# The context's up product in native fp32, and the S5 table sums moved from GpSimd to VectorE

## The chip, the core and the metric

The kernel runs on one core of one Trainium2 chip. The metric is the device time of one execution in microseconds (us), taken as the median of several runs. Engines are named as the profile names them: PE is the matrix engine (TensorE) and PEld its weight loads, DVE is VectorE, ACT is ScalarE, POOL is GpSimd, SP is SyncE, whose queue starts nearly all DMA transfers.

## What is computed

One layer over 1024 latent tokens and 256 context tokens, model width 1024, hidden width 2816. The part that matters is the first half-step SwiGLU on the context tokens, and the tables of the S5 scan that are built beside it:

```python
def half_step_ffn(x, mods, g_pre, g_post, w_gu, w_down):
    shift, scale, gate = mods
    h = modulate(rms_norm(x, g_pre), shift, scale)
    g, u = jnp.split(h @ w_gu, 2, axis=-1)
    y = (jax.nn.silu(g) * u) @ w_down
    return x + 0.5 * gate * rms_norm(y, g_post)
...
x = half_step_ffn(x, mods[0:3], ...)          # latent tokens
ctx = half_step_ffn(ctx, mods_c[0:3], ...)    # context tokens
```

The S5 tables are complex products of powers of `lam_bar` with the input matrix B and the output matrix C (`s5_discretise`, `s5_states` and `s5_readout` in the reference). They are needed later, by the scan over the latent tokens.

## The kernel before

The work runs in stages. First the latent up product (`g_lat`), then the context's up product (`g_ctx`, line 980), then the latent down product (`d_lat`, line 794), the context's down product, the mixer with the S5 pairs, and the second half-step. Side work is given out in small steps between the main steps: each main loop calls `step` (line 122), which advances a generator. During `g_ctx` that generator is `prep` (line 1760): 15 steps of `s5_prep` (line 1285), then loads of stored latent sums (`s_fetch`, seen as `z<-sd`), then the rest of `s5_prep`. The framework orders each engine's instructions by program order and by its own estimate of when they are ready; each engine, and SP's queue, then runs its list strictly in that order.

Matmuls mostly use a split scheme. `split` (line 157) turns an fp32 tensor into two tiles of type float32r: the high part is a rounded copy that ACT makes, the low part is the remainder, which DVE subtracts. `proj` (line 574) then makes each product of three matmuls: high by high, high by low, low by high.

`g_ctx` runs over 22 blocks of 128 hidden columns. For each block it needs two weight blocks of 1024 by 128 (512 KB each), one for the gate and one for the up half. `wcols` loads each into one of four buffers (`wrs`, tile `wr`), and splits it into two tiles of the pool `w` (six buffers, so three pairs). The raw buffer is free again once both halves of the split are made. With 8 blocks of the contraction, 22 blocks, two halves and three matmuls there are 1056 matmuls with 256 columns. The normalised context comes from `prenorm_g` (line 467), which splits it as well: `chi` and `clo`, four tiles of the pool `z`. Results leave through an ACT `Silu` and a DVE product, and are stored (`scd<-z`).

`s5_prep` makes four table blocks with `cmul` (line 1324: six DVE or POOL operations on 128x1024), and four with two groups of three (lines 1379 to 1386). Of each four, the odd ones run on POOL. After each `cmul` the matrix engine makes 16 small products with 32 columns, in native fp32, and 16 transposes. The tables go out as `pd<-z`, and the Toeplitz blocks through many small transfers, `gd<-z` and `td<-gd`. In the trace every recorded operation has line 51, which is a wrapper, so groups go by tile.

Of the kernel before, what the change touches and what calls it, by code (L numbers as in the profile page):

```python
# [10 lines left out]
F32R = mybir.dt.float32r  # L11
# [5 lines left out]
P = 128  # L17
D = 1024
KT = D // P
DFF = 2816  # L20
NF = DFF // P
NT = 1024
NC = 256
# [45 lines left out]
class Kernel:  # L69
# [397 lines left out]
    def prenorm_g(self, xs, a, b, hi, lo, wait=0):  # L467
        ss = self.t(self.sm, [P, 4], "ss")
        for k, x in enumerate(xs):
            self.square(ss, k, x)  # L470
            if k % SQ == SQ - 1:
                yield
        for _ in range(wait):
            yield
        r = self.rsq(ss[:, : len(xs)])
        yield
        for k, x in enumerate(xs):
            self.ts(x, x, r[:, k : k + 1])
            if k % SQ == SQ - 1:
                yield  # L480
        for _ in range(wait):
            yield
        _, one = self.blocks(xs, a, b)
        for kt in range(KT):
            h = self.t2()[:, : len(xs) * P]
            one(kt, h)
            self.split(hi(kt), lo(kt), h)
            yield

    def hop(self, x):  # L490
# [486 lines left out]
            t0 += n  # L977


    def g_ctx(self, wgu, hi, lo, fills):  # L980
        cols = lambda f: [self.wcols(wgu, f * P + q * DFF) for q in range(2)]
        nxt = cols(0)
        for f in range(NF):
            ws = nxt
            if f + 1 < NF:
                nxt = cols(f + 1)
            self.step(fills)
            if f % 4 == 0:
                s = self.z([P, 4, NC])
            pg, pu = self.ps(), self.ps()  # L990
            self.proj(pg[:, :NC], ws[0], hi, lo)
            self.proj(pu[:, :NC], ws[1], hi, lo)
            sg = self.t2()[:, :NC]
            self.nc.scalar.activation(sg, pg[:, :NC], AF.Silu)
            self.mul(s[:, f % 4, :], sg, pu[:, :NC])
            if f % 4 == 3 or f == NF - 1:
                n = (f % 4 + 1) * NC
                self.load(self.scd[f // 4][:, :n], s.rearrange("p k n -> p (k n)")[:, :n])
# [286 lines left out]
    def s5_prep(self):  # L1285
        nc, i = self.nc, self.i
        pl = nc.gpsimd
        slot = lambda shape: self.t(self.zp, shape, "z")
        crs = [slot([P, 4, 2, 64]) for _ in range(2)]
        for k, nme in enumerate(("ssm_c_re", "ssm_c_im")):  # L1290
            for d in range(2):
                self.load(crs[k][:, :, d, :], i[nme][0, d].rearrange("(b g) h p -> (g h) b p", b=4))
        pw, br_ = slot([P, 2, 2, T8, 32]), slot([P, 2, 32, H])
        self.load(pw.rearrange("p w r t a -> p (w r t a)"), self.pwd)
        self.load(br_.rearrange("p r a h -> p (r a h)"), self.brd)
        yield
        czp = [slot([P, 32, 2, H]) for _ in range(2)]
        ct = slot([P, 2, 32, H])
        for k in range(2):
            pl.memset(czp[k], 0.0)  # L1300
        for _ in range(4):
            yield
        for k in range(2):
            pt = self.ps()
            for b in range(4):
                self.tr(pt[:, b * P : (b + 1) * P], crs[k][:, b].rearrange("p d n -> p (d n)"), P)
            self.ts(ct[:, k].rearrange("p a h -> p (a h)"), pt, 1.0 - 2 * k)
            for d in range(2):
                r = slice(64 * d, 64 * d + 64)
                nc.scalar.activation(czp[k][r, :, d, :], ct[r, k], AF.Copy)  # L1310
            yield
        kt_ = slot([P, G, 32])
        pdv = self.pd.rearrange("a p w -> p a w")
        shp = [P, 8, T8, H]

        def power(w, r, gs):
            return pw[:, w, r, :, gs].rearrange("p t a -> p a t").unsqueeze(3).to_broadcast(shp)

        for o in range(4):
            gs = slice(8 * o, 8 * o + 8)  # L1320
            xr, xi, xt = slot(shp), slot(shp), slot(shp)
            b0 = br_[:, 0, gs, :].unsqueeze(2).to_broadcast(shp)
            b1 = br_[:, 1, gs, :].unsqueeze(2).to_broadcast(shp)
            self.cmul(xr, xi, power(0, 0, gs), power(0, 1, gs), b0, b1, xt, pl if o % 2 else None)
            yield
            pk = self.ps()
            for a in range(8):
                for r, xx in ((0, xr), (1, xi)):
                    nc.tensor.matmul(
                        pk[:, 32 * a : 32 * a + 32],  # L1330
                        xx[:, a].rearrange("p t h -> p (t h)"),
                        czp[r][:, 8 * o + a].rearrange("p q h -> p (q h)"),
                        start=r == 0,
                        stop=r == 1,
                    )
            nc.vector.tensor_copy(kt_[:, gs, :], pk[:, :256].rearrange("p (a n) -> p a n", n=32))
            yield
            for r, xx in ((0, xr), (1, xi)):
                ev = slot([P, 8, P])
                for b in range(2):  # L1340
                    pt = self.ps()
                    for a in range(4):
                        self.tr(
                            pt[:, a * P : (a + 1) * P],
                            xx[:, 4 * b + a].rearrange("p t h -> p (t h)"),
                            P,
                        )
                    nc.scalar.activation(
                        ev[:, 4 * b : 4 * b + 4, :], pt.rearrange("p (a n) -> p a n", n=P), AF.Copy
                    )  # L1350
                c0 = BO + 256 * r
                self.load(
                    pdv[:, 4 * o : 4 * o + 4, c0 : c0 + 256], ev.rearrange("p (a q) n -> p a (q n)", q=2)
                )
                yield

        lag0 = slot([H, G, H])
        self.load(lag0, kt_[112:128, :, 0:H])
        self.add(lag0, lag0, kt_[0:16, :, H:])
        for t in range(T8):  # L1360
            r = slice(t * H, t * H + H)
            if t < 7:
                self.load(self.gd[:, :, 14 - t], kt_[r, :, 0:H])
            if t > 0:
                self.load(self.gd[:, :, 7 - t], kt_[r, :, H:])
        self.load(self.gd[:, :, 7], lag0)
        yield
        for t in range(T8):
            r = slice(t * H, t * H + H)
            self.load(self.td[r], self.gd[:, :, 7 - t : 15 - t].rearrange("h g l k -> h g (l k)"))  # L1370
            if t % TY == TY - 1:
                yield
        for o in range(4):
            gs = slice(8 * o, 8 * o + 8)
            mr, mi, xt = slot(shp), slot(shp), slot(shp)
            prb, pib = power(1, 0, gs), power(1, 1, gs)
            cr_ = ct[:, 0, gs, :].unsqueeze(2).to_broadcast(shp)
            ci_ = ct[:, 1, gs, :].unsqueeze(2).to_broadcast(shp)
            e = pl if o % 2 else None
            self.mul(mr, cr_, prb, e)  # L1380
            self.mul(xt, ci_, pib, e)
            self.add(mr, mr, xt, e)
            yield
            self.mul(mi, ci_, prb, e)
            self.mul(xt, cr_, pib, e)
            self.sub(mi, mi, xt, e)
            for r, m in ((0, mr), (1, mi)):
                c0 = CO + 256 * r
                self.load(
                    pdv[:, 4 * o : 4 * o + 4, c0 : c0 + 256], m.rearrange("p (a q) t h -> p a (q t h)", q=2)  # L1390
                )
            yield
# [218 lines left out]
    def run(self):  # L1611
        nc, i = self.nc, self.i
# [3 lines left out]
        xs = i["x"][0].rearrange("(c t) d -> t c d", t=T8)  # L1616
# [7 lines left out]
        xt = [self.z() for _ in range(4)]  # L1624
# [32 lines left out]
        pt = self.ps()  # L1657
# [12 lines left out]
        h = self.hops(stages, bl, hb)  # L1670
# [35 lines left out]
        q, a = norm2(), accs2()  # L1706
# [30 lines left out]
            yield from self.s5_params()  # L1737

        hc = []
        chi = lambda k: hc[k // 4][:, k % 4, :]  # L1740
        clo = lambda k: hc[2 + k // 4][:, k % 4, :]

        def side():
            ct = [self.z() for _ in range(2)]
            for b in range(2):
                self.load_block(ct[b], cblk(b))
            hc.extend(self.z([P, 4, NC], dt=F32R) for _ in range(4))
            yield from self.prenorm_g(ct, self.modc[1, 1], self.modc[0, 1], chi, clo, 3)

        self.fill = fill()  # L1750
        self.lag = 0
# [19 lines left out]

        self.floor = ()
        self.fill = prep()
        self.g_ctx(i["ffn1_w_gu"][0], chi, clo, FC)
        self.drain()


# [184 lines left out]
        p = evac(2, acc)  # L1962
# [70 lines left out]
FC = 2  # L2033
# [53 lines left out]
```

## Time and profile before

| | |
|---|---|
| median of 3 runs | 2115.37 us (2113.56 to 2116.61) |
| profiled execution | 2112.9 us |
| span in its trace, first to last instruction | 2111.1 us |
| mean granted clock of TensorE | 0.964 of full speed |
| PE busy | 91% of the span |
| DVE, ACT, POOL busy | 77%, 39%, 11% of the span |
| `g_ctx`, first to last matmul | about 542.6 to 720.2 us from the start |

The profile comes from one execution. Its busy shares are means over stages, so a change in one stage has to be read from that stage's window. The time of a matmul in a group is longer than its share of the engine, since matmuls overlap; the spacing in a dense run tells its price.

### The profile page before, as it was taken

To read this page: it belongs to the slowest core of one execution; us is meant where nothing else is said; L and a number is where in the kernel's file an instruction comes from. 1 tells how busy PE (TensorE), PEld (TensorE's weight loads), DVE (VectorE), ACT (ScalarE), POOL (GpSimd) and SP (SyncE) were. 2 spreads that over 40 slices of the span, in tenths; PEclk is the share of its full clock that TensorE was granted. 3 is DMA by queue.
4 is the path that set the end of the run, shared out by engine and by line. 5 is a ranking of instruction groups with operands and counts; after the bars stand their busy time and mean duration, and the time that the engine had idled before them with its cause. 6 is when DMAs were issued, how large, how long until landed. Compare 5 with 4: busy or idle time off the path is not lost.

```text
span 2111.1 us, 25392 instructions
## 1 busy us (share of the span) xinstructions
PE 1913.8 (91%) x9018; PEld 1589.2 (75%) x9018; DVE 1631.6 (77%) x2791; ACT 816.2 (39%) x1416; POOL 228.8 (11%) x136
## 2 busy tenths in 40 slices
PE   5789898898899979999998789998799999999997
PEld 4568776686899857877887578886688888887775
DVE  6789998998866878798549998478875555577977
ACT  5433222333333334566531113337233333334443
POOL 0000000051336200000003552010000000000000
PEclk9989999999999999999999999999899999999999
DMA  8357552244579979276684443233552222167554
GB/s 301 99 161 238 161 181 78 86 154 150 170 216 271 348 285 309 88 267 250 184 241 169 146 141 114 69 104 116 167 185 88 90 90 82 64 254 273 206 184 160
DMA packets 338443, 366.20 MB, mean 173 GB/s; under 512 B 43216, under 2 KB 250764, under 8 KB 338316
## 3 DMA queue, kind: packets, MB, share of 16 engines
q1 hardware_dynamic: 336012, 356.19, 51.6%
q10 hardware_dynamic: 2304, 8.39, 1.0%
q8 instruction: 71, 1.16, 0.2%
q14 instruction: 56, 0.46, 0.1%
HBM read 293.45 MB, written 73.12 MB: 174 GB/s over the span
## 4 chain that ended last, share of the span: by engine, by line
PE 54%; DVE 30%; DMA 7%; issue 4%; ACT 3%; POOL 1%; SPq 1%; DVEq 0%; ACTq 0%; POOLq 0%
PE ps L51 54%; DVE t L51 11%; DVE z L51 7%; DVE w L51 6%; DVE tb L51 5%; DMA wr<-in_ffn_w_gu 2%; DMA wr<-in_ffn_w_down 1%; DMA tb<-in_w_ada 1%; ACT w L51 1%; ACT z L51 1%; ACT t L51 1%; DMA z<-sd 1%; SPq L51 1%; DVE sy L51 0%; DVE red L51 0%
## 5 line engine op out<-in xcount | busy, mean ns | idle before, releaser
L51 PE MATMUL ps<-z,w 128*128 128x512 f32 (+1 forms) x5712 | 1241.0, 378 | 94.4 <-ACT w L51 43.8
L51 PEld LDWEIGHTS ps<-z,w 128*128 128x128 f32 x5712 | 1016.7, 194 | 296.4 <-ACT w L51 50.1
L51 PE MATMUL ps<-w,w 128*128 128x512 f32 x1848 | 430.7, 393 | 18.8 <-DVE w L51 14.4
L51 PEld LDWEIGHTS ps<-w,w 128*128 128x128 f32 x1848 | 346.8, 189 | 99.9 <-DVE w L51 22.0
L51 ACT ACTIVATE w<-wr 128x512 fp32r<-128x512 f32 (+1 forms) x286 | 215.3, 758 | 375.4 <-PE ps L51 289.7
L51 DVE TENSOR_TENSOR w<-wr,w 128x512 fp32r<-128x512 f32 (+1 forms) x280 | 258.7, 929 | 86.1 <-ACT w L51 78.6
L51 ACT ACTIVATE w<-t 128x512 fp32r<-128x512 f32 x308 | 187.2, 627 | 289.2 <-DVE t L51 206.7
L51 DVE TENSOR_TENSOR w<-t,w 128x512 fp32r<-128x512 f32 x308 | 212.0, 698 | 60.0 <-ACT w L51 59.7
L51 DVE TENSOR_TENSOR t<-t,ps 128x512 f32<-128x512 f32 x150 | 102.2, 683 | 59.7 <-PE ps L51 59.2
L51 ACT ACTIVATE w<-z 128x512 fp32r<-128x512 f32 x110 | 69.3, 630 | 147.4 <-PE ps L51 143.8
L51 DVE TENSOR_TENSOR t<-wr 128x512 f32<-128x512 f32 x148 | 99.7, 686 | 29.0 <-DMA wr<-in_ffn_w_down 13.5
L51 ACT ACTIVATE t<-ps 128x512 f32<-128x512 f32 (+2 forms) x135 | 73.7, 548 | 108.4 <-PE ps L51 107.0
L51 DVE TENSOR_TENSOR z<-z,z 128x512 fp32r<-128x512 f32 (+3 forms) x127 | 104.9, 860 | 9.3 <-ACT z L51 5.0
L51 DVE SCALAR_TENSOR_TENSOR tb<-tb,scol 128x1024 f32<-128x1024 f32 x77 | 98.0, 1281 | 9.3 <-DMA tb<-in_w_ada 9.1
L51 DVE TENSOR_TENSOR w<-z,w 128x512 fp32r<-128x512 f32 x110 | 75.6, 688 | 27.4 <-ACT w L51 27.0
L51 POOL TENSOR_TENSOR z<-z,z 128x1024 f32<-128x1024 f32 x24 | 84.5, 3539 | 80.6 <-PE ps L51 44.9
L51 ACT ACTIVATE t<-z 128x1024 bf16<-128x1024 f32 (+3 forms) x132 | 75.2, 605 | 43.6 <-DVE z L51 30.3
L51 ACT ACTIVATE t<-t 128x512 f32<-128x512 f32 (+1 forms) x81 | 50.6, 625 | 104.6 <-DVE t L51 99.4
L51 PE MATMUL ps<-z,t 128*128 128x512 f32 x384 | 87.8, 389 | 1.1 <-ACT t L51 1.1
L51 PEld LDWEIGHTS ps<-z,t 128*128 128x128 f32 x384 | 72.0, 188 | 16.4 <-ACT t L51 1.5
L51 POOL TENSOR_TENSOR tb<-tb 128x512 f32<-128x512 f32 x24 | 34.9, 1465 | 447.9 <-DVE w L51 428.7
L51 ACT ACTIVATE z<-z 128x512 fp32r<-128x512 f32 (+2 forms) x76 | 47.9, 672 | 71.8 <-DVE z L51 66.1
(122 smaller groups left out, 1418.6 us busy)
## 6 DMA issues: line engine op xcount, KB each, us to landing
wr<-in_ffn_w_gu SPq DMA_DIRECT2D x156, 512.0 KB, 4.4
wr<-in_ffn_w_down SPq DMA_DIRECT2D x198, 256.0 KB, 4.1
tb<-in_w_ada SPq DMA_DIRECT2D x64, 512.0 KB, 4.7
sd<-z SPq DMA_DIRECT2D x44, 512.0 KB, 4.8
z<-sd SPq DMA_DIRECT2D x88, 256.0 KB, 5.2
z<-in_w_ada SPq DMA_DIRECT2D x24, 512.0 KB, 6.3
wr<-in_ffn_w_down SPq DMA_DIRECT2D x22, 512.0 KB, 4.9
wr<-in_w_in SPq DMA_DIRECT2D x20, 512.0 KB, 3.8
```

The source lines that it names most:

```text
L51: r = f(*a, **kw)
```

## The change

The context's up product takes the fp32 weights and the fp32 activations directly: one native fp32 matmul in place of three float32r ones, no split of the weights and none of the normalised context. The weights are read by the matmuls out of the four `wr` buffers. In `s5_prep` the odd table blocks now run on DVE like the even ones. (POOL keeps its blocks in `s5_params`, line 1248, and its work elsewhere.)

```diff
@@ prenorm_g
         for kt in range(KT):
-            h = self.t2()[:, : len(xs) * P]
+            h = hi(kt) if lo is None else self.t2()[:, : len(xs) * P]
             one(kt, h)
-            self.split(hi(kt), lo(kt), h)
+            if lo is not None:
+                self.split(hi(kt), lo(kt), h)
@@ g_ctx
-    def g_ctx(self, wgu, hi, lo, fills):
-        cols = lambda f: [self.wcols(wgu, f * P + q * DFF) for q in range(2)]
-        nxt = cols(0)
+    def g_ctx(self, wgu, h, fills):
+        def cols(f, q):
+            raw = self.wr().rearrange("p (k n) -> p k n", n=P)
+            c0 = f * P + q * DFF
+            self.load(raw, wgu[:, c0 : c0 + P].rearrange("(k p) n -> p k n", p=P))
+            return raw
+
+        nxt = [cols(0, q) for q in range(2)]
         for f in range(NF):
             ws = nxt
             if f + 1 < NF:
-                nxt = cols(f + 1)
+                nxt = [cols(f + 1, q) for q in range(2)]
             self.step(fills)
...
-            self.proj(pg[:, :NC], ws[0], hi, lo)
-            self.proj(pu[:, :NC], ws[1], hi, lo)
+            for pt, w in ((pg, ws[0]), (pu, ws[1])):
+                for kt in range(KT):
+                    self.nc.tensor.matmul(pt[:, :NC], w[:, kt, :], h(kt), start=kt == 0, stop=kt == KT - 1)
@@ s5_prep
-            self.cmul(xr, xi, power(0, 0, gs), power(0, 1, gs), b0, b1, xt, pl if o % 2 else None)
+            self.cmul(xr, xi, power(0, 0, gs), power(0, 1, gs), b0, b1, xt)
...
-            e = pl if o % 2 else None
+            e = None
@@ run
-        chi = lambda k: hc[k // 4][:, k % 4, :]
-        clo = lambda k: hc[2 + k // 4][:, k % 4, :]
+        ch = lambda k: hc[k // 4][:, k % 4, :]
...
-            hc.extend(self.z([P, 4, NC], dt=F32R) for _ in range(4))
-            yield from self.prenorm_g(ct, self.modc[1, 1], self.modc[0, 1], chi, clo, 3)
+            hc.extend(self.z([P, 4, NC]) for _ in range(2))
+            yield from self.prenorm_g(ct, self.modc[1, 1], self.modc[0, 1], ch, None, 3)
...
-        self.g_ctx(i["ffn1_w_gu"][0], chi, clo, FC)
+        self.g_ctx(i["ffn1_w_gu"][0], ch, FC)
```

## Rows read from the trace of the kernel before

**Rows 1.** The page's first part: busy time, share and instructions of the engines.
```profile
PE 1913.8 (91%) x9018; PEld 1589.2 (75%) x9018; DVE 1631.6 (77%) x2791; ACT 816.2 (39%) x1416; POOL 228.8 (11%) x136
```

**Rows 2.** Busy time by stretch: PE, PEld, DVE, ACT, POOL, clock, DMA share, GB/s.
```profile
542.60:720.20 177.60, 162.22 (x1274) 159.40 (x1273) 123.54 (x104) 63.62 (x88) 84.46 (x24) 0.94 0.80 245
588.47:591.70 3.23, 3.23 (x17) 3.23 (x18) 0.42 (x1) 0.00 (x0) 1.88 (x1) 0.53 0.87 277
608.50:611.50 3.00, 3.00 (x17) 3.00 (x17) 3.00 (x5) 0.60 (x1) 0.00 (x0) 0.51 0.67 196
660.00:680.00 20.00, 16.15 (x116) 15.33 (x115) 19.69 (x21) 5.01 (x7) 20.00 (x1) 0.91 1.01 285
...
760.00:780.00 20.00, 14.62 (x58) 12.03 (x59) 13.13 (x22) 4.50 (x8) 0.00 (x0) 0.78 0.64 244
```

**Rows 3.** What PE waited for, 542 to 721 us: total, times, longest.
```profile
PE ps L51 <- DVE w L51: 11.2, 6, 7.0
PE ps L51 <- ACT w L51: 4.1, 3, 2.5
```

**Rows 4.** Groups by form, 542.6 to 720.2 us: busy, mean ns, idle before.
```profile
L51 PE MATMUL ps<-z,w 128*128 128x256 f32 x1056 | 142.1, 295 | 15.4 <-DVE w L51 11.2 <-ACT w L51 4.1
L51 POOL TENSOR_TENSOR z<-z,z 128x1024 f32<-128x1024 f32 x24 | 84.5, 3539 | 80.6 <-PE ps L51 44.9 <-DMA z<-brd 21.1 <-DVE z L51 12.6
L51 DVE TENSOR_TENSOR w<-wr,w 128x1024 fp32r<-128x1024 f32 x43 | 70.6, 1649 | 26.8 <-ACT w L51 25.4 <-DMA z<-in_ssm_c_re 1.3
L51 ACT ACTIVATE w<-wr 128x1024 fp32r<-128x1024 f32 x42 | 44.5, 1059 | 91.9 <-PE ps L51 71.7 <-DMA wr<-in_ffn_w_gu 12.2 <-issue 3.5
L51 DVE TENSOR_TENSOR z<-z,z 128x1024 f32<-128x1024 f32 x24 | 37.2, 1580 | 0.0
```

**Rows 5.** DVE's order of time, 555 to 580 us: start, length, count.
```profile
559.41 9.34 DVE L51 TENSOR_TENSOR z<-z,z 128x1024 f32<-128x1024 f32 x3
568.67 3.35 DVE L51 TENSOR_TENSOR w<-wr,w 128x1024 fp32r<-128x1024 f32 x1
...
576.28 1.21 DVE L51 TENSOR_TENSOR z<-z,z 128x1024 f32<-128x1024 f32 x1
```

**Rows 6.** Dense runs of matmuls in PE's order of time: start, length, count.
```profile
605.12 3.43 PE L51 MATMUL ps<-z,z 128*128 128x32 f32 x30
...
703.06 17.30 PE L51 MATMUL ps<-z,w 128*128 128x256 f32 x142 [1.48 <-DVE w L51]
...
1114.87 1.25 PE L51 MATMUL ps<-tb,z 128*128 128x160 f32 x8
```

**Rows 7.** PE's instructions written from the small matmuls' PSUM tiles, same stage.
```profile
L51 PE MATMUL ps<-z,z x128: 194/276/401, 576.9 to 647.0; 128*128 128x32 f32 x128
L51 PE MATMUL ps<-ident,z x72: 270/272/454, 557.8 to 651.0; 128*128 128x128 f32 x72
```

**Rows 8.** DMA issues, 650 to 720 us: count, size, us from issue to landing.
```profile
wr<-in_ffn_w_gu SPq DMA_DIRECT2D x14, 512.0 KB, 6.2
```

**Rows 9.** SP's queue in order of time, 645 to 672 us: start, length, count.
```profile
645.69 0.63 SPq L51 DMA_DIRECT2D wr<-in_ffn_w_gu  x1
647.73 3.77 SPq L51 DMA_DIRECT2D gd<-z  x5
...
660.38 0.56 SPq L51 DMA_DIRECT2D wr<-in_ffn_w_gu  x1
...
662.35 1.39 SPq L51 DMA_DIRECT2D wr<-in_ffn_w_gu  x2
664.89 6.38 SPq L51 DMA_DIRECT2D td<-gd  x8
671.37 1.69 SPq L51 DMA_DIRECT2D wr<-in_ffn_w_gu  x1
```

**Rows 10.** What PE waited for, 510 to 543 us.
```profile
PE ps L51 <- DVE t L51: 0.4, 1, 0.4
```

**Rows 11.** What PE waited for, 740 to 770 us.
```profile
PE ps L51 <- DVE red L51: 9.5, 1, 9.5
```

## The prediction

> **What bounds the kernel now.** I read the page's busy shares first: PE is busy 91% of the span, DVE 77%, POOL 11% [rows 1]. That only says that PE is the engine to watch. The changed lines run in one stage, so the second view is the busy time of the stretch from the first matmul of the context's up product to the end of its last, 177.6 us long: PE is busy 162.2 of them, DVE 123.5, POOL 84.5 [rows 2]. The third view is what PE waited for there: 11.2 us on DVE's low parts of weights and 4.1 on ACT's high parts, 15.4 in all with rounding [rows 3]. So this stage is PE's with a few holes. What is taken from DVE, ACT and POOL can give back the holes and no more; what is added to PE's work is paid in full. The fourth view, the groups by form, says what fills the engines: 1056 matmuls of 256 columns on PE, and on DVE 43 subtractions at a mean of 1.65 us [rows 4]. DVE's order of time tells why they are that slow: while POOL works, three operations take 9.34 us and the subtraction behind them 3.35; without POOL the same 128x1024 operation takes 1.21 [rows 5]. PE's longest wait, 7.0 us, ends with that late subtraction.
>
> PE's busy time is not all work at full speed. Dense runs give the price of one matmul as the spacing, with 0.295 for the last one [rows 4]: (17.30 - 0.295) / 141 = 0.1206 us for a float32r matmul of 256 columns [rows 6]. 1056 of them are 127.4 us. The native products with 32 columns go at (3.43 - 0.28) / 29 = 0.109 [rows 6, 7]; 128 records are 14.0, and I put the 72 transposes at the same price, 7.8. The 18 other matmuls of the stretch, most of them 512 columns wide at about 0.23, make 4.1. The sum is 153.3 against 162.2 busy, so some 8.9 us went to a lowered clock. It shows: right after two groups of the small products the granted clock is 0.53 and 0.51 for 3.23 and 3.00 us, which is 1.2 GHz in place of 2.4, a loss of 0.47 x 3.23 + 0.49 x 3.00 = 3.0. Around the waits at 665 us it is 0.91 over 20 us, a loss of 1.8 [rows 2]; the rest of the 8.9 lies around the other holes.
>
> **The change, part by part.** *The matmuls.* A native fp32 product appears in the trace as two records: the 64 small products of the S5 tables in the program are 128 records [rows 7]. So 352 products become 704 records of 256 columns. No such size is in the trace. The nearest row is native with 160 columns: (1.25 - 0.295) / 7 = 0.136 us [rows 6], which is two cycles a column at 2.4 GHz (0.133) plus 0.003. With 256 columns that gives 0.213 + 0.003 = 0.216, and 704 x 0.2164 = 152.3. Lower end: no overhead, 0.2133, 150.2. Upper end: the overhead that the float32r matmul has over one cycle a column, 0.1206 - 0.1067 = 0.0139, falls on each native record too: 0.2272, 160.0. I take 0.2164, as the row is of the same kind. PE's work grows by 152.3 - 127.4 = **24.9 us** (22.8 to 32.6). The loads of the weights stay hidden: with 32 columns a record takes 0.109, load and all, which is half of 0.216. If they did not hide, 704 x 0.109 = 77 would come on top, but the 160-column row has its loads in it and shows none of that.
>
> Weighed against a rule: the 160-column row shows four cycles a column for one product, in two records, while three float32r matmuls need three plus 0.014 us each [rows 6]. The Trainium skill ("FP8 and Floating Point Precision", TensorE Precision Notes) says that true fp32 makes four passes through the array. It speaks against this change: four passes in place of three, counted as passes alone, are 352 x 256 columns at 2.4 GHz, an estimate of 37.5 us more. By the rows it is 24.9, since native saves the overhead of three matmuls. The sum goes by the rows.
>
> *The splits.* 44 subtractions leave DVE and 44 copies leave ACT. Off PE's path they are worth nothing; on it they are the 15.4 us of waits. *The sums.* 24 operations leave POOL (3.54 each, 84.5) and go to DVE at 1.21, 29.0 us [rows 4, 5]; DVE's other 24 fall from 37.2 to about 29 as POOL is silent. DVE then has 123.5 - 70.6 + 29.0 - 8.2 = 73.7 us of work in a stage of some 190, so the moved sums cost nothing: PE's 178 us of work cover them. Six in a row (7.3 us) hold back the product that frees a PSUM bank, but eight banks stand against two used in 6.9 us. With that cover gone the price would be up to 29.0.
>
> *The weights' buffers.* This is where a new wait comes from. Today a raw buffer is free once it is split, so four raw and three split pairs stand ahead of PE, seven weight blocks of 24 x 0.1206 = 2.9 us. After the change only the four raw ones do, each held until its 16 records (3.46 us) are done. From the release of a buffer to the use of its next content there are 3 x 3.46 = 10.4 us. A load lands 6.2 us after its issue in the busy part of the stage [rows 8], so 4 us are left. SP's queue takes more than that at two places: between the loads of weights at 645.69 and 660.38 it issues other transfers, mostly `gd`, without a weight among them (14.7 us), and the `td` transfers hold the next one from 662.35 to 671.37 (9.0) [rows 9]. If the queue stays so, PE waits 14.7 + 6.2 - 10.4 = 10.5 and 9.0 + 6.2 - 10.4 = 4.8, together 15.3; if loads come between, none. I take the middle, 8. A load that waits for PE also holds back what is behind it on SP's queue: table stores, `gd` and `td`, the stored sums `z<-sd`, and the first weights of the latent down product. Only the last two are needed at the end of the stage. The first of those weights goes into a buffer that is free 10.4 us ahead and lands in 6.2, so I put this at nothing; it is 6.2 at the most, one landing.
>
> *Before the stage.* Eight small splits fewer in `prenorm_g`, and two `z` tiles fewer: PE waits only 0.4 us between 510 and 543 [rows 10], with the latent up product ahead of it, so nothing is to be had.
>
> *The sum.* Work +24.9. Waits 15.4 to 8: -7.4. Clock: the 3.0 behind the small products stay, 1.8 for the remaining waits, so 8.9 to 4.8: -4.1. Together **+13.4**: 2112.9 + 13.4 = 2126.3 for the profiled execution. The median of the runs is 2.5 above that execution, so 2128.8.
>
> **Rivals.** *Nothing comes back (later still).* The weight loads come as late as worked out, 15.3 us of waits take the place of the 15.4, and the clock falls as now: +24.9, 2140.3; with the upper price 2147.9. For it: the seven blocks ahead today could not cover SP's long gap, and four are fewer. Against it: the queue's order is made anew, and a weight is then asked for every 3.46 us.
>
> *All holes close (no change).* Weights are always there, and no wait is left: +24.9 - 15.4 - (8.9 - 3.0) = +3.6, 2119.0, within 0.2% of before, which is 4.2 us and about what a measurement of this kernel can tell from no change. For it: PE's waits all name split work that goes away. Against it: SP's gaps [rows 9], and ACT itself often waited for the loads of weights, 12.2 us [rows 4].
>
> *DVE sets the pace (faster).* What DVE does too late is the real limit, also beyond the stage: at the start of the latent down product PE waits 9.5 us for a DVE reduction [rows 11], and the clock is 0.78 over the next 20 us, 4.4 lost [rows 2]. If a freed DVE runs ahead there too, 15.4 + 5.9 + 9.5 + 4.4 = 35.2 come back against 24.9: 10.3 less, 2105.1. It decides once over 29.1 of the 35.2 come back. For it: DVE is nearly full up to that wait. Against it: that reduction sums modulation loads that are issued only with that stage's own, so a DVE idle earlier has nothing of it to do.
>
> That the change doesn't do what it says (no native product) I leave out: small ones are in the trace.
>
> **How the numbers follow.** The forecast (+4.2 to +19, 2119.6 to 2134.5) has 0.47, nothing back 0.17, all holes closed 0.18, DVE's pace 0.18. Slower by over 0.2% is the first two, 0.64; within 0.2% 0.18; faster 0.18. The range 2108 to 2141 leaves out about 0.12 of DVE's case and 0.08 of the late weights with the upper price. The point is the forecast's own time, 2128.8.
>
> **What would show it.** In the profile after: 704 records of 256 columns, spaced 0.216 in a dense run; a stage of about 191 us where it is 177.6 now; PE's waits naming the DMA of `wr`, about 8 us, and none naming `w`; DVE near 74 us busy and no POOL in it; the clock halved only behind the small products. The prediction is wrong if the spacing is far from 0.216, if the waits on `wr` are near zero or above 15, or if the stages behind move by more than 5 us, as the whole order is planned anew.

## The result and the profile after

The changed kernel takes 2142.35 us, the median of 4 runs (2135.23 to 2144.36), where the kernel before takes 2115.99 beside it (4 runs, 2113.56 to 2119.01). The ratio is 1.0124, with a 95% interval of 1.0106 to 1.0141: slower by 26.4 us. The direction was forecast, the size was not: +13.4 was said, and 2142.35 lies just above the stated range, which ended at 2141. Measured once more beside other kernels it was 2138.67 (2135.83 to 2141.20), ratio 1.0103 (1.0081 to 1.0124), so the move is 24 to 26 us.

The profiled execution of the changed kernel spans 2138.8 us. The first part of its page, which answers to [rows 1]:

```profile
PE 1944.2 (91%) x8666; PEld 1599.7 (75%) x8666; DVE 1577.2 (74%) x2763; ACT 771.4 (36%) x1364; POOL 144.7 (7%) x112
```

PE is busy for 30.4 us more with 352 instructions fewer, and DVE, ACT and POOL have less to do. Where the time went is seen in the busy times by stretch. The columns are those of [rows 2], and the first line is the stage of the context's up product, from its first matmul to the end of its last:

```profile
547.20:736.30 189.10, 179.80 (x916) 157.87 (x915) 72.76 (x85) 22.98 (x47) 0.00 (x0) 0.98 0.73 219
...
580.00:620.00 40.00, 40.00 (x228) 35.88 (x228) 12.22 (x15) 6.68 (x13) 0.00 (x0) 1.00 0.61 185
...
680.00:700.00 20.00, 14.48 (x55) 12.13 (x56) 20.00 (x21) 0.77 (x2) 0.00 (x0) 0.83 1.04 304
716.30:736.30 20.00, 20.00 (x94) 17.64 (x93) 3.54 (x7) 3.45 (x7) 0.00 (x0) 1.00 0.74 232
736.30:756.30 20.00, 17.81 (x78) 14.17 (x77) 16.99 (x22) 5.99 (x10) 0.00 (x0) 1.00 1.02 380
756.30:776.30 20.00, 14.70 (x56) 10.69 (x55) 19.51 (x33) 5.72 (x10) 0.00 (x0) 0.91 1.02 384
776.30:796.30 20.00, 13.13 (x46) 10.15 (x46) 14.58 (x23) 6.21 (x13) 0.00 (x0) 0.75 0.84 315
```

The stage is 189.1 us long where it was 177.6 [rows 2]. DVE has fallen from 123.5 to 72.8 us of work in it, and in the last 20 us of the stage it is nearly idle (3.5 us). Right behind the stage it is nearly full again, and PE is the one that stands. That edge, at 736.3 us, matters below.

What PE waited for inside the stage, 547 to 737 us (in us: total, times, longest), which answers to [rows 3]:

```profile
PE ps L51 <- DMA wr<-in_ffn_w_gu: 7.5, 4, 5.2
PE ps L51 <- DVE z L51: 1.8, 1, 1.8
```

And the groups by form there, which answer to [rows 4]:

```profile
L51 PE MATMUL ps<-z,wr 128*128 128x256 f32 x703 | 163.7, 386 | 7.5 <-DMA wr<-in_ffn_w_gu 7.5
...
L51 DVE TENSOR_TENSOR z<-z,z 128x1024 f32<-128x1024 f32 x48 | 56.1, 1214 | 0.2
...
L51 PE MATMUL ps<-z,z 128*128 128x32 f32 x128 | 16.6, 259 | 1.8 <-DVE z L51 1.8
```

A group's mean of 386 ns is not the price of a record, since pipelined matmuls overlap. The spacing is, and it is read from dense runs in PE's order of time, as in [rows 6] (start, length, count):

```profile
555.09 8.79 PE L51 MATMUL ps<-z,wr 128*128 128x256 f32 x40
...
692.66 44.03 PE L51 MATMUL ps<-z,wr 128*128 128x256 f32 x192 [5.15 <-DMA wr<-in_ffn_w_gu]
```

With 0.386 for the last record, (8.79 - 0.386) / 39 = 0.2155 us. The second run stands behind a wait of 5.15 us, and there the clock is 0.83 over 20 us; 192 records at 0.2155 would be 41.4, so the lowered clock behind that wait cost about 2.6.

To find the rest, the span is cut at points that all these kernels have: GpSimd's first tensor operation, which lies ahead of the first changed instruction on PE, DVE, ACT and POOL, the first matmul of the latent down product (`ps<-w,w`), and the first of the context's down product (`ps<-w,t`). The starts are read from the order of time on POOL and PE. The kernel before was profiled three times (the second and third are experiments below), the changed one twice:

| us | ahead of the mark | mark to `d_lat` | `d_lat` | from the context's down product to the end |
|---|---|---|---|---|
| before | 430.0, 429.3, 432.4 | 290.2, 290.2, 288.2 | 243.1, 245.3, 243.9 | 1147.8, 1152.0, 1149.1 |
| changed | 433.8, 432.5 | 302.5, 303.1 | 249.2, 248.8 | 1153.3, 1152.8 |
| difference of means | +2.6 | +13.3 | +4.9 | +3.4 |

The four differences make 24.2. The forecast of +13.4 belongs to the second column, the only one in which it placed a cost. The other 10.9 us were not in it.

**Theory.** The stage itself costs about what was predicted, and the late start of the latent down product is a second cost of the same change: the native product holds the four `wr` buffers until PE is done with them, so the weights of the next stage come late. **Rivals.** The moved sums cost something; SP's queue is held by bursts of small transfers or by loads of stored sums, and not by the buffers; and the offset ahead of the mark belongs to the changed program rather than to one execution.

### The profile page after: what moved, and what is told of

It reads as the page before. It is cut to its first block, busy times and chain, and to the rows that moved or that the text cites. A ratio compares the mean times of both kernels' runs of the same rounds, so it can differ in the third digit from the quotient of the medians.

```text
span 2138.8 us, 24520 instructions
## 1 busy us (share of the span) xinstructions
PE 1944.2 (91%) x8666; PEld 1599.7 (75%) x8666; DVE 1577.2 (74%) x2763; ACT 771.4 (36%) x1364; POOL 144.7 (7%) x112
## 4 chain that ended last, share of the span: by engine, by line
PE 60%; DVE 25%; DMA 7%; issue 4%; ACT 2%; SPq 1%; POOL 1%; DVEq 0%; ACTq 0%; POOLq 0%
PE ps L51 60%; DVE t L51 10%; DVE z L51 6%; DVE w L51 4%; DVE tb L51 4%; DMA wr<-in_ffn_w_down 2%; DMA wr<-in_ffn_w_gu 1%; DMA tb<-in_w_ada 1%; SPq L51 1%; ACT z L51 1%; ACT w L51 1%; ACT t L51 1%; DMA z<-pd 1%; DVE sy L51 0%; POOL t L51 0%
## 5 line engine op out<-in xcount | busy, mean ns | idle before, releaser
L51 PE MATMUL ps<-z,w 128*128 128x512 f32 (+1 forms) x4656 | 1104.5, 398 | 79.0 <-ACT w L51 37.4
L51 PEld LDWEIGHTS ps<-z,w 128*128 128x128 f32 x4656 | 885.1, 193 | 279.5 <-ACT w L51 42.6
L51 ACT ACTIVATE w<-wr 128x512 fp32r<-128x512 f32 (+1 forms) x242 | 168.8, 703 | 297.8 <-PE ps L51 218.3
L51 DVE TENSOR_TENSOR w<-wr,w 128x512 fp32r<-128x512 f32 (+1 forms) x236 | 186.0, 793 | 70.6 <-ACT w L51 64.5
L51 PE MATMUL ps<-z,wr 128*128 128x256 f32 x704 | 164.0, 386 | 7.5 <-DMA wr<-in_ffn_w_gu 7.5
L51 PEld LDWEIGHTS ps<-z,wr 128*128 128x128 f32 x704 | 131.3, 193 | 26.6 <-issue 9.0
L51 DVE TENSOR_TENSOR z<-z,z 128x512 fp32r<-128x512 f32 (+3 forms) x151 | 123.3, 856 | 23.0 <-DMA z<-z 17.4
L51 DVE TENSOR_TENSOR z<-t,ps 128x512 f32<-128x512 f32 (+1 forms) x52 | 29.7, 571 | 120.0 <-PE ps L51 119.2
L51 ACT ACTIVATE z<-ps 128x512 f32<-128x512 f32 x74 | 41.8, 596 | 127.1 <-PE ps L51 122.1
```

The lines of the kernel that those rows point to most:

```text
L51: r = f(*a, **kw)
```

## The experiments

**The changed kernel once more** (`after_again`; no edit).

> The changed kernel itself, unaltered, for a second profile of it: how far its stages repeat. Its first profile was 27.7 us longer than that of the kernel before: 3.7 us lay ahead of the first changed instruction, 11.6 in the context's up product (189.2 against 177.6 us), 6.1 in the latent down product, 5.6 behind it. Theory A (PE's work and late buffers): the stage and the first 50 us of the latent down product repeat within 2 us, and the 3.7 ahead and the 5.6 behind go to within 3 of zero, as chance of one execution. Rival B (the rest of the kernel is slower in a lasting way, by order or place of buffers): the 3.7 and the 5.6 are there again. Time 2138 to 2146 us by both.

2138.67 us, ratio 1.0103 (1.0081 to 1.0124). The stage and `d_lat` repeat within 0.6 us (table above). The offsets ahead of the mark and at the end became smaller, but did not vanish, so this run alone left them open.

**Native product, sums back on GpSimd** (`fp32_pool`): one half of the change without the other.

```diff
-            self.cmul(xr, xi, power(0, 0, gs), power(0, 1, gs), b0, b1, xt)
+            self.cmul(xr, xi, power(0, 0, gs), power(0, 1, gs), b0, b1, xt, pl if o % 2 else None)
...
-            e = None
+            e = pl if o % 2 else None
```

> Native fp32 product as in the changed kernel, but the odd table blocks back on GpSimd: the product's part alone. Order on PE differs from the changed kernel only inside the stage. Theory A: PE's work sets the stage, the sums lie under it on either engine, so 2142 within 4 us. Rival C (the moved sums cost the time, by making DVE late): most of the loss goes away, under 2130. Rival D (GpSimd slows DVE and the tables come late, so that PE waits for the small products): 5 to 15 us more, over 2147.

2137.69 us, ratio 1.0093 (1.0068 to 1.0118), the changed kernel's time. The stage is 303.0 from the mark, `d_lat` 248.8, and PE waits 8.0 us on the weights. With the native product, it makes no difference on which engine the sums run: the rival of the moved sums is out.

**Sums on VectorE, splits kept** (`split_dve`): the other half alone, so the kernel before with only the two lines of `s5_prep` changed.

```diff
-            self.cmul(xr, xi, power(0, 0, gs), power(0, 1, gs), b0, b1, xt, pl if o % 2 else None)
+            self.cmul(xr, xi, power(0, 0, gs), power(0, 1, gs), b0, b1, xt)
...
-            e = pl if o % 2 else None
+            e = None
```

> The kernel before with the odd table blocks on DVE: the other part alone, three float32r matmuls and the splits kept. Theory A: DVE has 43 x 1.21 + 48 x 1.21 = 110 us of work in 177 and no longer slows to 3.1 us an operation beside GpSimd, so the 7.0 us wait at 565 us and part of the others go: 5 to 12 us less than before, 2104 to 2111. Rival C (sums on DVE make it late): equal to before or slower, 2116 to 2125.

2113.59 us (10 runs, 2108.25 to 2115.78), against 2114.65 of before: ratio 0.9988 (0.9976 to 1.0000). The stage is 281.2 from the mark, 7 to 9 us shorter than before; `d_lat` stays at 244.1. The time fell between the two expectations: the stage's gain is there, but this profile reaches the mark only at 434.05 us and takes 1152.1 from the context's down product on, so little of the gain is left in the whole. Twice as many sums on DVE cost nothing, since every one of them is fast when GpSimd is silent. DVE's groups in this kernel's stage, against the 1.58 and 1.65 us of [rows 4]:

```profile
L51 DVE TENSOR_TENSOR z<-z,z 128x1024 f32<-128x1024 f32 x48 | 56.5, 1213 | 0.0
L51 DVE TENSOR_TENSOR w<-wr,w 128x1024 fp32r<-128x1024 f32 x42 | 51.1, 1219 | 20.5 <-ACT w L51 17.4 <-DMA wr<-in_ffn_w_gu 1.7 <-PE ps L51 1.3
```

It has the lowest median of all the kernels here, though its gain over the kernel before, 1 us, is at the edge of what 10 runs can tell. The whole loss of the change is the native product's.

**Deeper buffers for half the weights** (`fp32_deep`): the up half's weights go to the pool `w`, which the splits have left free.

```diff
-            raw = self.wr().rearrange("p (k n) -> p k n", n=P)
+            raw = self.wt([P, KT, P], dt=F32) if q else self.wr().rearrange("p (k n) -> p k n", n=P)
```

> The changed kernel with the up half's weights loaded into the six buffers of the pool w, which it leaves unused in this stage, and the gate half's into the four raw ones: ten weight blocks deep in place of four. Theory A: PE's waits on weight loads (7.5 us, with a clock fall of 2 to 3 behind the longest) go, and the first weights of the latent down product are loaded earlier, so its slow start (6.1 us) comes back too: 10 to 16 us less than the changed kernel, 2126 to 2132, and still over the kernel before by the rest of PE's added work. Rival B (the rest is slower in a lasting way): only the waits in the stage go, 2133 to 2138. Rival E (loads are not late for want of buffers but for SP's transfers of tables): no change, 2140 to 2145.

2133.44 us, ratio 1.0079 (1.0058 to 1.0101). What PE waited for in the stage, and then in the first 100 us of `d_lat`:

```profile
PE ps L51 <- DVE z L51: 1.8, 1, 1.8
...
PE ps L51 <- DVE red L51: 9.6, 1, 9.6
PE ps L51 <- DVE w L51: 6.9, 2, 5.1
PE ps L51 <- DVE z L51: 4.3, 1, 4.3
```

No wait for weights is left in the stage, which is 291.4 from the mark, 11 shorter. But `d_lat` takes 254.0, 5 longer: a part of what the stage gained comes back as waits on DVE at the start of the next one. So theory A held for the stage, and its claim that the slow start of `d_lat` would go as well did not. A reading that fits, though no line shows it directly: the weights in `w` are held until PE is done as well, and the high and low parts of the next stage's weights need tiles of that same pool.

**The kernel before, unchanged** (`before_again`).

> The kernel before, unaltered, for a second profile. All five later profiles show 2.5 to 4.1 us more than its first one ahead of the first changed instruction, and 2.3 to 3.5 more behind the last reordered one (226.6 us then, 228.9 to 230.1 since), though the instructions there stand in the same order. Theory A (chance of that one execution, which was a short one): the two stretches take about 433 and 229 us here, and the median of before is 2 to 4 us above the first profile. Rival B (a lasting effect of the change outside the changed stage): 430 and 226.6 again.

2118.61 us in one run. It reaches the mark at 429.3 us, so the offset of the changed kernel looked lasting here; from the context's down product on it takes 1152.0, 4 us longer than the first profile of the same program. The third profile of before, at the end of this section, changed the first of these readings.

**Stored sums on ACT's queue** (`fp32_actq`, and the same edit on `split_dve` and `fp32_deep`): if the 33 loads `z<-sd` hold what is behind them on SP's queue, they should cost less elsewhere.

```diff
+        ld = self.nc.scalar.dma_start if m == 2 and sd is self.sd[0] else self.paced
...
-            self.paced(st[j][:, :512], sd[j][:, :512])
+            ld(st[j][:, :512], sd[j][:, :512])
```

> The changed kernel with the 33 loads of stored sums that the second product of the latent down product needs issued from ACT's queue, not SP's, where they stand behind loads of weights that wait for a buffer. Theory F (the late start of those loads is what the latent down product loses: in the last 20 us of the stage the DMA engines are 0.74 busy and after it 1.02 for 40 us): they run under the context's up product, the latent down product takes 235 to 243 us in place of 249, and the total falls by 6 to 14, to 2126 to 2134. Rival G (its start is bound by DVE or by the volume of all transfers, whenever they begin): 247 to 251 us there, total 2137 to 2143. Rival H (more transfers under the stage make its weights late): the stage grows by 5 or more and takes the gain away.

> The kernel before with the sums on DVE (split_dve) and the same 33 loads on ACT's queue. Theory F: the latent down product falls from 244 us by 5 to 12, total 2100 to 2108, faster than both kernels. Rival G: 2111 to 2116. Rival H: over 2116, since ACT makes the high parts of weights here and would wait in front of a load.

> fp32_deep (ten weight blocks) with the same 33 loads on ACT's queue: both late things removed from the native version. fp32_deep gained 11 us in the stage and gave 5 back at the start of the latent down product (254 us). Theory F: that falls to 237 to 243, total 2118 to 2124: what is left over before is PE's added work less the waits that it lost. Rival G: 2130 to 2136, unchanged.

None became faster. The first two are slower than without the edit: 2148.12 us, ratio 1.0178 (1.0144 to 1.0212), and 2120.73, 1.0030 (1.0009 to 1.0051). The third has 2136.28, 1.0115 (1.0089 to 1.0140), 2.8 us over `fp32_deep`, but the two intervals overlap. `d_lat` grew to 254.1, 252.9 and 257.4. ACT's order of time in the first of them, ACTq being ACT's own DMA issues:

```profile
739.95 6.90 ACTq L51 DMA_DIRECT2D z<-sd  x5
746.90 0.63 ACT L51 ACTIVATE w<-z 128x512 fp32r<-128x512 f32 x1 [7.45 <-DMA z<-sd]
```

Five issues, with waits between them, stretch over 6.9 us, and the split behind them began right after the last, when ACT had stood idle for 7.45 us. The profile names the landing of such a load as what it waited for. The theory that these loads are what makes the start of `d_lat` late fell, or at least this edit can't show it: it puts a new wait in front of the splits.

**The Toeplitz transfers on ACT's queue** (`fp32_tdact`): 22 of the 23 transfers `gd` and `td` leave SP's queue; PE's order is that of the changed kernel.

```diff
-                self.load(self.gd[:, :, 14 - t], kt_[r, :, 0:H])
+                nc.scalar.dma_start(self.gd[:, :, 14 - t], kt_[r, :, 0:H])
...
-            self.load(self.td[r], self.gd[:, :, 7 - t : 15 - t].rearrange("h g l k -> h g (l k)"))
+            nc.scalar.dma_start(self.td[r], self.gd[:, :, 7 - t : 15 - t].rearrange("h g l k -> h g (l k)"))
```

> The changed kernel with the small transfers of the Toeplitz blocks (gd and td, 23 of them) issued from ACT's queue, which has little to do in this stage, not from SP's; PE's order is the changed kernel's to the last instruction. Theory E (weights are late because SP issues these transfers between them, with only four buffers to bridge it): PE's waits on weight loads fall from 7.2 to 7.5 us to under 2, the stage from 189 to 179 to 183 us, the latent down product stays at 249, total 6 to 11 us less than the changed kernel, 2129 to 2135. Rival K (four buffers are too few whatever the queue does): waits stay over 5 us, total 2137 to 2143.

2134.31 us, ratio 1.0091 (1.0074 to 1.0107). PE's waits in the stage:

```profile
PE ps L51 <- DMA wr<-in_ffn_w_gu: 3.9, 3, 2.8
PE ps L51 <- DVE z L51: 1.8, 1, 1.8
```

The waits on weights fall from 7.5 to 3.9 and the stage is 2.3 to 2.9 shorter, so about half of the waits went with these transfers. That lies between theory E (under 2) and rival K (over 5): both causes seem to have a part. The whole time is not clearly below the changed kernel's, since the intervals overlap. The changed kernel's queue shows the place (SP's order of time):

```profile
677.93 0.39 SPq L51 DMA_DIRECT2D wr<-in_ffn_w_gu  x1
680.69 5.90 SPq L51 DMA_DIRECT2D td<-gd  x8
686.69 4.07 SPq L51 DMA_DIRECT2D wr<-in_ffn_w_gu  x3
```

Eight `td` transfers stand between two loads, and PE waits until 692.66 for the later one: 6.0 us after its issue. `d_lat` is 248.9 as before this edit, so the late start of the next stage has another cause.

**The last four blocks' weights in other buffers** (`fp32_zlast`): eight of the 44 weight loads go to `z` tiles, so that the `wr` buffers are free earlier for the next stage.

```diff
-            raw = self.wr().rearrange("p (k n) -> p k n", n=P)
+            raw = self.z([P, KT, P]) if f >= NF - 4 else self.wr().rearrange("p (k n) -> p k n", n=P)
```

> The changed kernel with the weights of its last four blocks in tiles of the pool z; the four raw buffers are then free some 25 us before the end of the context's up product. Theory J (the latent down product begins late because its first loads wait for raw buffers that the native product holds until PE is done, and DVE, which has some 50 us of work up to the second modulation sum, starts that work late): it takes 241 to 245 us in place of 249, total 4 to 8 less than the changed kernel or more where waits in the stage go as well, 2130 to 2136. Rival G (the volume of transfers or DVE's work decides, not their start): 248 to 251 there, total 2137 to 2143.

2133.04 us (2128.42 to 2138.11), ratio 1.0088 (1.0068 to 1.0109), inside the 2130 to 2136 expected if held buffers are the cause. The interval overlaps that of the changed kernel's second measurement, so the reading rests on the stages. The last 20 us of the stage and the first 20 of `d_lat`, to be laid beside the lines 716.30 and 736.30 of the changed kernel:

```profile
719.00:739.00 20.00, 20.00 (x96) 17.60 (x94) 9.10 (x10) 1.78 (x4) 0.00 (x0) 1.00 1.05 360
739.00:759.00 20.00, 20.00 (x91) 16.49 (x90) 16.95 (x31) 7.10 (x13) 0.00 (x0) 1.00 1.05 409
```

The DMA engines are full at the stage's end (1.05 in place of 0.74), DVE has begun (9.1 us of work in place of 3.5), and PE has no hole in the first 20 us of `d_lat`. `d_lat` takes 240.7 where it took 249, and the stage before it is about 1 longer. From the mark to the context's down product it is 544.7 where the changed kernel has 551.7 and 551.9: 7 us. The waits on weights in the stage, 7.8 on `wr` and 1.1 on the new buffers, have not become less.

That the weights of `d_lat` come late, and no longer do here, is seen on ACT, which makes their high parts. What ACT waited for in the first 54 us of `d_lat`, in the kernel before, in the changed one and in this one:

```profile
ACT w L51 <- DMA wr<-in_ffn_w_down: 14.6, 6, 4.0
...
ACT w L51 <- DMA wr<-in_ffn_w_down: 24.4, 7, 6.9
...
ACT w L51 <- DMA wr<-in_ffn_w_down: 6.5, 3, 4.0
```

The other profiles of the first two kernels show 11.0, 12.4 and 26.2.

**Both** (`deep_zlast`): the weights of the last four blocks in `z`, those of the up half ahead of them in `w`.

```diff
-            raw = self.wr().rearrange("p (k n) -> p k n", n=P)
+            raw = self.z([P, KT, P]) if f >= NF - 4 else self.wt([P, KT, P], dt=F32) if q else self.wr().rearrange("p (k n) -> p k n", n=P)
```

> Ten buffers as in fp32_deep, and the last four blocks in z tiles as in fp32_zlast, so that neither raw buffers nor those of the pool w are held at the end. By theories E and J together: stage 178 us as in fp32_deep, latent down product 241 to 246 in place of that kernel's 254, total 2117 to 2124: PE's added work with all holes closed, and no faster than before. If the latent down product stays at 250 or more, theory J is wrong for this kernel: 2128 to 2134.

2119.39 us (7 runs, 2114.30 to 2123.77), ratio 1.0016 (0.9998 to 1.0035): 20 us of the loss are gone. From the mark to the context's down product it takes 533.6, against 533.3, 535.5 and 532.1 in the three profiles of before. What PE waited for in the stage, and in the first 100 us of `d_lat`:

```profile
PE ps L51 <- DMA z<-in_ffn_w_gu: 4.5, 1, 4.5
PE ps L51 <- DVE z L51: 1.8, 1, 1.8
...
PE ps L51 <- DVE z L51: 4.2, 1, 4.2
PE ps L51 <- DVE red L51: 2.8, 1, 2.8
PE ps L51 <- DVE w L51: 1.5, 1, 1.5
```

Alone the two edits gave 6.4 and 7.1 us over these two stages; together they give 18.2. The parts differ from the expectation: the stage is 185.6 us long from its first matmul, where 178 was expected, and `d_lat` 234.5, where 241 to 246 was. ACT waits only 0.4 us for the weights in the first 54 us of `d_lat`. Why the two gains together are more than their sum is not shown; a reading that fits is that each edit alone leaves the buffers short at one of two places. But with both, the native product still only draws level with the splits: `split_dve` needs 525.3 for the same two stages.

**The kernel before, a third profile** (`before_third`), on the offset ahead of the mark.

> The kernel before, unchanged, one look. It asks where the 3 to 5 us come from by which every changed kernel so far reaches GpSimd's first tensor operation later (431.3 to 435.0 us against 430.0 and 429.3), although each engine's order is the same up to there. In the two profiles of before, the run of 60 matmuls that starts at 42 to 43 us takes 13.9 us at a granted clock of 1.00; in the changed kernel it takes 16.3 and 15.5 us with a clock of 0.50 and 0.58 over 44 to 48 us. If the lowered clock is a chance of the execution, it may show here as well: the run takes 15.4 us or more and GpSimd's first operation comes at 431 us or later. If it goes with the program, the run takes 13.9 us and the operation comes at 429 to 430.5 us. One profile can show the first, and can only add one case to the second.

2115.42 us in one run. In the traces of the kernel before and of the changed one, PE, DVE, ACT, GpSimd and SP's queue keep the same order until some 523 us into the span, and the offset has arisen by 81 us. The same 60 matmuls in PE's order of time, first in the first profile of before:

```profile
43.21 13.88 PE L51 MATMUL ps<-z,w 128*128 128x512 f32 x60
```

then in the changed kernel:

```profile
43.70 16.32 PE L51 MATMUL ps<-z,w 128*128 128x512 f32 x60
```

and in this third profile of before:

```profile
43.26 15.52 PE L51 MATMUL ps<-z,w 128*128 128x512 f32 x60
```

The busy times of the stretch from 44 to 48 us in the first profile of before, with the granted clock in the third column from the right:

```profile
44.00:48.00 4.00, 4.00 (x19) 3.32 (x18) 0.95 (x2) 4.00 (x9) 0.00 (x0) 1.00 0.45 133
```

and in the third:

```profile
44.00:48.00 4.00, 4.00 (x12) 3.09 (x11) 1.15 (x3) 4.00 (x8) 0.00 (x0) 0.57 0.45 133
```

The unchanged program shows the lowered clock too, in one of its three profiles, and then reaches the mark at 432.4. So a good part of the +2.6 can be the chance of an execution. Not all of it need be: `deep_zlast` had the clock at 1.00 there, and reached the mark at 433.0 nevertheless.

## Why the prediction came out half right

**The price of a record: right.** 0.2155 measured, 0.2164 predicted. 704 records are 151.7, so the product costs 24.3 more, where 24.9 was forecast. The stage's work, put together as in the forecast with 128 small products, 72 transposes and 13 wide matmuls, is 151.7 + 14.0 + 7.8 + 3.0 = 176.5 against 153.3: 23.2, since five wide matmuls fewer fall into the stage. The weight loads stayed hidden. The rule weighed there, that true fp32 makes four passes (the Trainium skill, "FP8 and Floating Point Precision", TensorE Precision Notes), agrees with the spacing: two records of 256 columns at 0.2155 are 4.04 cycles a column at 2.4 GHz. Counted as passes alone it would have made +37.5, which is not what the stage shows.

**Waits: nearly right, in part by luck.** PE's waits fell from 15.4 to 9.3, of which 7.5 name the DMA of `wr`, against 8 forecast. The mechanism was also the one named, four raw buffers and transfers between the loads on SP's queue; half the waits went when these left the queue. But the 8 was only the middle between none and 15.3, and the parts came out otherwise: the `gd` transfers were to cost the most, 10.5, and the longest wait by far, 5.2, stands behind the `td` burst. The 1.8 on a DVE result before the small products wasn't foreseen.

**Clock: the term was mis-sized in the safe direction.** Busy time less work is 179.8 - 176.5 = 3.3, where it was 8.9 and 4.8 was forecast. The forecast kept 3.0 behind the small products. There is nothing there: 580 to 620 us runs at 1.00, where [rows 2] has 0.53 and 0.51. Most of what is left, 2.6, stands behind the wait that ends at 692.66 us, as forecast for the waits.

**The stage.** 23.2 - 6.1 - 5.6 = 11.5, which is the 189.1 against 177.6. The forecast was +13.4, a stage of 191, so it was nearly 2 too high there. The 13.3 counted from the mark comes closer, but it takes in some 113 us ahead of the stage and the spread of the profiles: the first two alone differ by 12.3. DVE's work there was put at 74 and is 72.8; no wait names `w`.

**The step that failed: "I put this at nothing; it is 6.2 at the most, one landing."** That was said of the first weights of the latent down product. The measured price is 4.9 us in `d_lat`, out of the 11 to 13 by which the forecast fell short. The step looked at one buffer and one landing. What was late was a whole queue. SP's order at the end of the stage, in the kernel before (`d_lat` begins at 720.2):

```profile
705.30 3.64 SPq L51 DMA_DIRECT2D wr<-in_ffn_w_down  x3
...
709.71 1.73 SPq L51 DMA_DIRECT2D wr<-in_ffn_w_down  x2
711.47 1.04 SPq L51 DMA_DIRECT2D tb<-in_w_ada  x2
```

and in the changed one (`d_lat` begins at 736.3):

```profile
710.96 12.32 SPq L51 DMA_DIRECT2D wr<-in_ffn_w_gu  x5
723.43 0.47 SPq L51 DMA_DIRECT2D scd<-z  x1
724.63 8.62 SPq L51 DMA_DIRECT2D wr<-in_ffn_w_down  x7
733.30 0.90 SPq L51 DMA_DIRECT2D tb<-in_w_ada  x2
```

The last up loads wait for PE: the final three of the five go out at 716.00, 719.45 and 722.91, 3.45 us apart, which is the time of 16 records at 0.2155. The first down load follows 11.7 us ahead of `d_lat` instead of 14.9, and seven down loads instead of five stand in front of the modulation loads. So these go out 3.0 us ahead of `d_lat` instead of 8.7. DVE, which is busy for 51 of the 60 us behind that edge (the three lines from 736.30 on), begins late by it. DVE's order of time in the kernel before:

```profile
715.79 0.68 DVE L51 TENSOR_TENSOR w<-wr,w 128x512 fp32r<-128x512 f32 x1
717.49 1.28 DVE L51 SCALAR_TENSOR_TENSOR tb<-tb,scol 128x1024 f32<-128x1024 f32 x1 [1.02 <-DMA tb<-in_w_ada]
```

and in the changed one, where DVE is idle ahead of the first split and again ahead of the third:

```profile
729.62 0.69 DVE L51 TENSOR_TENSOR w<-wr,w 128x512 fp32r<-128x512 f32 x1 [6.21 <-ACT w L51]
...
737.62 0.69 DVE L51 TENSOR_TENSOR w<-wr,w 128x512 fp32r<-128x512 f32 x1 [4.60 <-ACT w L51]
738.23 1.28 DVE L51 SCALAR_TENSOR_TENSOR tb<-tb,scol 128x1024 f32<-128x1024 f32 x1
```

The first modulation product starts 2.7 us before `d_lat` in the kernel before and 1.9 after its start in the changed one, 4.6 later. The reduction on which PE then waits starts 43.9 us into `d_lat` (764.11) before and 48.1 (784.43) after, 4.2 later. That it was the held buffers and not the number of transfers is shown by `fp32_zlast`: with other buffers for the last eight weight blocks, and as many transfers, the stage's end fills up, ACT's wait for the weights falls to 6.5 us, and `d_lat` loses 8 us. (SP's order was made anew there as well, so the two extra loads in front of the modulation are not told apart from the buffers.) The reason that the step gave, a buffer free 10.4 us ahead and a landing in 6.2, holds for the first load alone, which went out 11.7 us ahead; the ones behind it had to wait for PE in turn.

The other 6.0 us of the shortfall, ahead of the mark and behind `d_lat`, lie where the forecast had no term; for them no failed step can be named beyond that, and their cause stays open (below). The forecast's own sign of being wrong, stages behind that move by more than 5 us, did appear: `d_lat` and what follows moved by 8.3 together.

**The rivals of the forecast.** "All holes close" is not what the change does, but it is what it can do: with both edits the kernel is at 2119.4, where 2119.0 was given for that case. It gets there by other terms, though, since a wait of 4.5 stays in the stage and `d_lat` gains. "DVE sets the pace" is refuted: DVE's load fell by 50 us in the stage and PE's wait on the reduction at the start of `d_lat` was still 6.9 us (9.1 in the second profile), with 5.8 more on ACT's split, which waits for the weights. "Nothing comes back" gave 2140.3, near the measured time, but by other terms: 11.7 us of holes and clock did come back, and 10.9 went to the stretches around the stage.

**What stays open.** The +3.4 behind `d_lat`. Before has 1147.8 to 1152.0 there, the changed kernel 1152.8 and 1153.3, and `split_dve`, which loses nothing overall, 1152.1. No run was made that touches it. Of the +2.6 ahead of the mark, the lowered clock at 44 us explains a part, and whether the rest is chance was not settled: `split_dve`, which loses nothing, reaches the mark at 434.05, later than the changed kernel.

## What to carry to other kernels

When products stop being split, their weights stay in the landing buffers for as long as PE computes on them; count what those buffers serve next, the stage behind included, and follow every transfer that is behind on the same queue. A step that moves work off an engine which is not the bottleneck pays only where that engine is late: DVE lost 50 us of work here, and the start of the next stage came later. And make the two parts of a change one at a time: the moved sums alone were level with or slightly better than the kernel before, and the native product alone cost all that was lost.

## What the runs showed of the hardware

- The same 60 matmuls of the same program took 13.9 us in one execution and 15.5 in another, with the granted clock at 1.00 and at 0.57 over 44 to 48 us, so 1.2 GHz for most of that stretch in place of 2.4. Ahead of it PE had two waits of about 1 us each and 16 products of one column, in both. A profile can thus differ by 1.6 us from the next one without any change in the program.
- Behind two groups of the small products with 32 columns the clock was halved in the kernel before (0.53 and 0.51, [rows 2]); in the changed one, where the same products stand between native records of 256 columns, it was 1.00 from 580 to 620 us.
- Transfers started from ACT's queue stood in the way of its own work: five issues, with the waits between them, stretched over 6.9 us, and the split behind them began right after the last, after 7.45 us without work.
